# Decoder trunk: operand sums, negated copies, one softmax scaling and one rotation table put in other places

## The chip, the cores and the metric

The kernel runs on one core of a Trainium2 chip. The metric is the device time of one execution in microseconds (us); the median of several runs counts. The engines are PE (TensorE: matmuls and transposes), DVE (VectorE), ACT (ScalarE), POOL (GpSimd) and SP (SyncE, here only a DMA queue). Each engine works through its own instruction queue in order; ACT, POOL and SP also issue DMAs from theirs.

## The reference, cut to what matters

One layer with two groups of eight heads on a sequence of 1024 tokens, model width 2048, all in float32:

```python
hn = rmsnorm(h, norm_mix_g)
sb_q, sb_k, sb_v, sb_g, df_q, df_k, df_v, df_g = split(hn @ w_in)
sb_out = stick_breaking_attention(sb_q, sb_k, sb_v)               # 8 heads of 128
dq, dk = partial_rope(df_q, pos), partial_rope(df_k, pos)
df_out = softmax1(dq, dk) @ df_v - lam * softmax2(dq, dk) @ df_v  # 8 heads, 2 x 64
df_out = rmsnorm(df_out, subln_g) * (1 - lambda_init)
mixed = concat([sb_out * silu(sb_g), df_out * silu(df_g)])
h = h + mixed @ w_out
gate = sigmoid(rmsnorm(h, norm_ple_g) @ w_ple_gate)
out = rmsnorm(h + gate * (p @ w_ple_proj), norm_final_g)
```

## The kernel before

Activations are kept transposed: features on partitions, tokens along the free axis, in two halves of 512 tokens (half 1 first, since attention is causal and the tokens stand in reverse order). Each float32 operand of a big product is split into a high part that TensorE can use exactly and a low rest. ACT makes the high part (a cast or a scaled copy), DVE the low part (source minus high part), and a product is three matmuls: high by high, high by low, low by high. So nearly every matmul needs one ACT step and then one DVE step to have been done.

The time falls into these parts:

- **The ramp, 0 to about 100 us.** The value and gate columns of `w_in` (16 units) are multiplied by a seven-product scheme on 2 x 2 blocks: A11, A12, S1 to S4 and A22 name the activation operands, of which S1 to S4 are sums and differences of blocks. The ramp does A11 and A12 for all units, two units at a time: A11 of both, then A12 of both. For each unit `load` fetches the weights and `cast` makes `wfh` (ACT, L714) and `wfl` (DVE, L715); the casts for the next two units stand behind the two A12 products. The other operands are formed in between: `todo` is a queue of 40 small steps (`combine`, `divide`, `split1`) that work on tiles `x`, and `some(n)` writes the next n of them into the queues of ACT and DVE at that place of the program.
- **The other products of this scheme**, to about 615 us.
- **Head units, about 615 to 1600 us.** For each half (1, then 0) and each of the 16 heads, in the order of `ORDER`: differential head 8, stick-breaking head 0, 9, 1, and so on to 15, 7. A unit makes q and k of one head with 96 matmuls (L295 to L297), in 32 groups of three. In between, the attention of the head before is run.
- **Output projection, gate, final norm**, from about 1600 us, again by seven products.

The order of the work in a unit is a table, `TICK`. After each group of three matmuls `side.tick()` counts on by one and writes out the steps whose time has come; `side.later(dt, fn)` puts a step dt ticks on. So a table entry moves a step along the queues of ACT and DVE, relative to the matmuls and to the other steps. PE, DVE and ACT keep exactly this order; the queues of POOL and SP are set by a scheduler.

At the **seam** between the halves, three things meet. The last units of half 1 end their attention. `mixed` stores each head's gated output `sg` and, for half 1, a negated copy `neg` (ACT, L327), which goes by DMA into the block sums for the output projection. And the activations of half 0 take the place of those of half 1: `swap(pc)`, at ticks 7, 15, 23 and 31 of the last unit, loads four tiles each, and `split` in `load_x0` makes `xh` (ACT, L1245) and `xl` (DVE, L1246) as many ticks later as `TICK["x0"]` says. In the same place the rotation table `cs` of half 0 (cosine and sine, 128 x 1024) is loaded by POOL and multiplied by the row norms on DVE (L1227). The table of half 1 is scaled in the same way near 642 us.

In the attention of a differential head, `weights` runs per block of 128 rows and per softmax c: `top` (DVE, L426) finds the row maximum of the scores `z`, `one` (ACT, L434) takes the exponential into `et`, and for c = 1 `two` scales `et` by lam over the row sum (DVE L439 and L440, then ACT L441), and `three` (DVE, L446) forms the difference, which PE then turns (L481, tile `tp`). ACT and DVE split the turned blocks into `awh` and `awl` (L500, L505; `lead` for the first block, L499, L504) for the product with the values (`av`, L523 to L528). A score tile `z` is free for the next scores when L434 has read it. The ticks of `top`, `one`, `two` and `three` are `TICK["df_soft"]`.

Of the kernel before, what the change touches and what calls it, by code (L numbers as in the profile page):

```python
# [17 lines left out]
ALU = mybir.AluOpType  # L18
AX = mybir.AxisListType

P = 128
D = 2048
S = 1024
HALF = 512
# [15 lines left out]
TICK = {  # L40
    "sumlag": 2, "gvx": ((22, 27), (80, 85)), "chore": (36, 78, 87), "opx": (8, 12), "turn": 76, "lag": 15, "gap": (4, 6),
    "parts": (1, 2), "vparts": (3, 4), "sums": (0, 2), "squared": (3, 4.5), "norm": (1, 4),
    "df_scores": (-20, -16, -13, -8, -4, 0, 4, 8), "df_turn": (19, 19), "df_v": -1, "df_norm": 44.5,
    "sb_scores": (-2, 5.5, 13.5, 22), "sb_turn": (32, 36), "sb_v": 23, "df_soft": (1, 1.5, 4, 5.5),
    "sb_stick": (1, 1, 3, 5.5), "taken": (28, 31), "sb_split": (1, 2), "kv": 9, "df_vg": (25, 37, 42, 58, 59.5),
    "sb_vg": (4, 15, 16, 24, 25.5), "q_turn": (-1.0, 5.5, 5, 6.5, 10, 12, 13.5),
# [5 lines left out]
    "begun": (86.5, 91.5, 93.5, 94.5, 93.5), "mid_turn": 76, "mid_lag": 17, "mid_gap": (4, 6),  # L52
    "mid_df_scores": (-20, -16, -9, -8.5, -1, -0.5, 4, 8), "mid_df_turn": (19, 17), "mid_df_v": -1, "mid_df_norm": 44.5,
    "mid_sb_scores": (-3, 5, 12.5, 21), "mid_sb_turn": (32, 36), "mid_sb_v": 22, "mid_taken": (28, 31),
    "mid_q_turn": (-1.5, 4.5, 4.5, 5.5, 9.5, 11.5, 12.5), "mid_k_turn": (-1.5, 8, 8.5, 9, 13.5, 15, 16, 17.5), "end_turn": 76,
    "end_lag": 15, "end_gap": (4, 6), "end_df_scores": (-23, -16, -15, -8, -4, 0, 4, 8), "end_df_turn": (18.5, 19),
    "end_df_v": -1, "end_df_norm": 44.5, "end_sb_scores": (-2, 6, 13.5, 22), "end_sb_turn": (32, 36), "end_sb_v": 23,
    "end_taken": (28, 31), "end_q_turn": (-1.0, 5, 5, 6.5, 10, 12, 13.5),
    "end_k_turn": (-4.5, 8, 8.5, 10, 13.5, 15, 16, 17.5),
}  # L60
# [9 lines left out]
def _body(ctx, nc, tc, ap):  # L70
# [247 lines left out]
    def mixed(half, hd, t):  # L318


        ph, second, i = hd % H // 4, hd < H, hd % 4
        S1, S2, S3, S4 = [comb_d[ph, j, i] for j in range(4)]
        if half == 1 or second:
            nc.sync.dma_start(mixed_d[half, hd], t)
        if half == 1:
            n = ev.tile([P, HALF], F32, name="neg", tag="xt", bufs=4)
            A.activation(n, t, AF.Copy, scale=-1.0)  # L327
# [12 lines left out]
        G.dma_start(S4, t, accum_op=ALU.add)  # L340


    def attention(at, pz, half, hd, q, qz, K, KL, VV, sg, vg, rcol):

        sb = hd < H
        nkey = HALF * len(K)
        nb = nkey // P
# [12 lines left out]
        def scores(c, rb):  # L360
# [29 lines left out]

            side.later(TICK["sb_stick"][0], masked)
            return z

        def weights(rb, c):
# [3 lines left out]
            if sb:  # L398
                def one():
                    pt = at.tile([P, S], F32, name="pt", tag="pt")  # L400
                    bt = row_block("bt", rb)
                    A.activation(pt[:, off + 1:nkey], z[:, off:nkey - 1], AF.Sigmoid, scale=rcol[:, 0, rb:rb + 1])  # L402
                    A.activation(bt[:, vw], z[:, vw], AF.Sigmoid, scale=rcol[:, 1, rb:rb + 1])
                    ws[rb] = pt, bt

                def two():
                    pt, bt = ws[rb]
                    w = slice(off + 1, nkey)
                    V.tensor_tensor_scan(pt[:, w], pt[:, w], pt[:, w], initial=1.0, op0=ALU.mult, op1=ALU.bypass)  # L409
# [6 lines left out]
                for dt, fn in zip(TICK["sb_stick"][1:], (one, two, three)):  # L416
                    side.later(dt, fn)
                return

            def top():  # L420
# [5 lines left out]
                V.tensor_tensor_reduce(z[:, vw], z[:, vw], add, -DF_SCALE, 3.0e38, ALU.add, ALU.min, mx)  # L426
                side.later(TICK["df_soft"][1], partial(one, mx))

# [58 lines left out]
        def parts(pr, g, tp, wh, wl):  # L487
# [18 lines left out]

            side.later(TICK["parts"][0], high)
            side.later(TICK["parts"][1], low)

        def mix(pr, g):  # L510
# [27 lines left out]
            av = sm.rearrange("p a b -> p (a b)")  # L538
            side.later(TICK["sums"][0], lambda: A.copy(sm[:, 1, :], av4[:, 3, :]))

# [6 lines left out]

            side.later(TICK["sums"][1], summed)
            if sb or pr == 0:
# [16 lines left out]

            side.later(TICK["squared"][0], squared)
            side.later(TICK["squared"][1], low)

# [51 lines left out]
    with tc.tile_pool(name="at", bufs=2) as at, tc.tile_pool(name="pz", bufs=2, space=PSUM) as pz:  # L621
# [313 lines left out]
        def some(n):  # L935
            for _ in range(n):
                if todo:
                    todo.popleft()()

        for u in range(0, NVG, 2):  # L940
            aa = [pp.tile([P, HALF], F32, name="pa", tag="acc", bufs=2) for _ in range(2)]
            for i in range(2):
# [20 lines left out]
                if u:  # L963
                    some(4)
            for i in range(2):
# [260 lines left out]
        def scale_rope(hf, cs):  # L1226
            V.tensor_tensor(cs, cs, rstds[hf].unsqueeze(1).to_broadcast([P, 2, HALF]), op=ALU.mult)  # L1227

# [178 lines left out]
        for half in (1, 0):  # L1407
            X = X0 if half == 0 else X1

            for hd in ORDER:  # L1410
# [15 lines left out]
                if half == 1 and hd == ORDER[-1]:  # L1426
# [3 lines left out]

                    side.add([(8 * pc + 7, partial(swap, pc)) for pc in range(4)])

# [107 lines left out]
                if half == 1 and hd == ORDER[-2]:  # L1540
                    cs = rope_of(0)
                    side.add([(27, partial(scale_rope, 0, cs))])
                if hd >= H:
# [860 lines left out]
```

## Time and profile before

| | us |
|---|---|
| median of 3 runs | 2325.04 (2324.98 to 2326.09) |
| the profiled execution, its own time | 2326.05 |
| its span from the first to the last instruction | 2324.3 |
| PE busy | 2306.5 |
| DVE busy | 1796.6 |
| ACT busy | 1269.1 |
| POOL busy | 326.1 |

The granted clock of TensorE was 0.999 in this execution. In rows of the timeline the columns are: start, duration, engine, line, operation, output <- inputs, shape, count; in brackets stands the time that the engine was idle just before, and what ended it. "PEld" is the loading of weights into the array, which runs beside the matmuls. "SPq" marks DMA issues.

### The profile page before, as it was taken

To read this page: it belongs to the slowest core of one execution; us is meant where nothing else is said; L and a number is where in the kernel's file an instruction comes from. 1 tells how busy PE (TensorE), PEld (TensorE's weight loads), DVE (VectorE), ACT (ScalarE), POOL (GpSimd) and SP (SyncE) were. 2 spreads that over 40 slices of the span, in tenths; PEclk is the share of its full clock that TensorE was granted. 3 is DMA by queue.
4 is the path that set the end of the run, shared out by engine and by line. 5 is a ranking of instruction groups with operands and counts; after the bars stand their busy time and mean duration, and the time that the engine had idled before them with its cause. 6 is when DMAs were issued, how large, how long until landed. Compare 5 with 4: busy or idle time off the path is not lost. (4 is left out here: it accounts for less than half of the span.)

```text
span 2324.3 us, 32653 instructions
## 1 busy us (share of the span) xinstructions
PE 2306.5 (99%) x11089; PEld 1928.1 (83%) x11089; DVE 1796.6 (77%) x3119; ACT 1269.1 (55%) x2303; POOL 326.1 (14%) x497
## 2 busy tenths in 40 slices
PE   9999999999999999999999999999999999999998
PEld 7888888888888888887888888888888888888887
DVE  7487776766578888877778878788787988687787
ACT  6323243333356677777776776667733435542555
POOL 2121111111211111100011001110121121111000
PEclk9999999999999999999999999999999999999999
DMA  7586788876888787888676667777899789998975
GB/s 265 201 303 227 253 280 220 222 160 129 208 265 259 242 255 246 253 287 284 203 214 186 182 207 207 205 200 243 259 216 242 248 248 282 309 358 267 299 255 187
DMA packets 258455, 556.66 MB, mean 239 GB/s; under 512 B 28896, under 2 KB 39392, under 8 KB 258288
## 3 DMA queue, kind: packets, MB, share of 16 engines
q1 hardware_dynamic: 180816, 366.55, 49.9%
q0 software_dynamic: 60912, 158.10, 25.7%
q10 hardware_dynamic: 16560, 29.92, 3.6%
q8 instruction: 87, 1.43, 0.2%
q14 instruction: 80, 0.66, 0.1%
HBM read 359.16 MB, written 203.69 MB: 242 GB/s over the span
## 5 line engine op out<-in xcount | busy, mean ns | idle before, releaser
L788 ACT CAST wpr<-T 128x512 fp32r<-128x512 f32 x208 | 127.1, 620 | 470.7 <-DVE T L747 393.7
L295 PE MATMUL acc<-xh,whi 128*128 128x512 f32 x768 | 312.9, 407 | 0.0
L297 PE MATMUL acc<-xh,wlo 128*128 128x512 f32 x768 | 301.1, 392 | 0.1
L296 PE MATMUL acc<-xl,whi 128*128 128x512 f32 x768 | 300.7, 392 | 0.0
L297 PEld LDWEIGHTS acc<-xh,wlo 128*128 128x128 f32 x768 | 144.2, 188 | 32.5 <-DVE wlo L196 0.5
L295 PEld LDWEIGHTS acc<-xh,whi 128*128 128x128 f32 x768 | 144.7, 188 | 24.5 <-issue 0.2
L296 PEld LDWEIGHTS acc<-xl,whi 128*128 128x128 f32 x768 | 144.9, 189 | 23.8 <-issue 0.2
L901 POOL DMA_DIRECT2D vg_d<-hc x128 | 89.1, 696 | 447.0 <-DVE hc L1119 263.4
L802 DVE TENSOR_TENSOR wpr<-T,wpr 128x512 fp32r<-128x512 f32 x208 | 142.6, 685 | 6.9 <-ACT wpr L788 3.8
L200 ACT CAST whi<-wraw 128x1024 fp32r<-128x1024 f32 x128 | 134.1, 1048 | 18.2 <-DMA wraw<-w_in 8.4
L788 ACT CAST wpr<-wraw 128x512 fp32r<-128x512 f32 x128 | 78.8, 617 | 105.1 <-DMA wraw<-tw_d 31.8
L434 ACT ACTIVATE et<-z,mx 128x512 f32<-128x512 f32 (+7 forms) x128 | 95.2, 744 | 60.3 <-DVE mx L426 60.2
L426 DVE CUSTOM_DVE_ANT_0 z<-z,wide 128x512 f32<-128x512 f32 (+7 forms) x128 | 97.6, 764 | 29.9 <-PE z L379 27.1
L505 DVE TENSOR_TENSOR awl<-tp,awh 128x256 fp32r<-128x256 f32 (+1 forms) x160 | 92.5, 578 | 33.9 <-ACT awh L500 33.0
L500 ACT CAST awh<-tp 128x256 fp32r<-128x256 f32 (+1 forms) x160 | 80.6, 504 | 43.7 <-PE tp L481 42.7
L802 DVE TENSOR_TENSOR wpr<-wraw,wpr 128x512 fp32r<-128x512 f32 x128 | 86.7, 685 | 16.4 <-ACT wpr L788 16.3
L409 DVE TENSOR_TENSOR_SCAN pt<-pt 128x511 f32<-128x511 f32 (+3 forms) x64 | 86.7, 1355 | 14.4 <-ACT pt L402 13.9
L196 DVE TENSOR_TENSOR wlo<-wraw,whi 128x1024 fp32r<-128x1024 f32 x56 | 68.5, 1224 | 14.2 <-ACT whi L200 13.7
L528 PE MATMUL av<-awl,v 128*128 128x256 f32 x256 | 72.6, 284 | 0.4 <-DVE awl L505 0.4
L526 PE MATMUL av<-awh,v 128*128 128x256 f32 x256 | 72.2, 282 | 0.5 <-ACT awh L500 0.4
L527 PE MATMUL av<-awh,v 128*128 128x256 f32 x256 | 72.2, 282 | 0.0
L441 ACT ACTIVATE et<-et,l 128x512 f32<-128x512 f32 (+3 forms) x64 | 49.4, 772 | 40.9 <-DVE l L440 40.8
(581 smaller groups left out, 6937.8 us busy)
## 6 DMA issues: line engine op xcount, KB each, us to landing
wraw<-w_in SPq DMA_DIRECT2D x128, 512.0 KB, 4.7
wraw<-w_vg SPq DMA_DIRECT2D x143, 256.0 KB, 3.8
vg_d<-hc POOLq DMA_DIRECT2D x128, 256.0 KB, 5.0
wlo_d<-wlo POOLq DMA_DIRECT2D x56, 512.0 KB, 6.4
wlo<-wlo_d SPq DMA_DIRECT2D x48, 512.0 KB, 3.8
wraw<-w_gate SPq DMA_DIRECT2D x92, 256.0 KB, 5.6
h_d<-hc POOLq DMA_DIRECT2D x56, 256.0 KB, 5.4
wraw<-w_out SPq DMA_DIRECT2D x56, 256.0 KB, 4.7
```

Of the source, the lines that this page charges most:

```text
L200: side.later(1, lambda: A.copy(hi[:, o], raw[:, o]))
L295: T.matmul(acc[c], hi[:, k2, kh, c, :], xh, start=first, stop=False)
L296: T.matmul(acc[c], hi[:, k2, kh, c, :], xl, start=False, stop=False)
L297: T.matmul(acc[c], lo[k2][:, kh, c, :], xh, start=False, stop=last)
L409: V.tensor_tensor_scan(pt[:, w], pt[:, w], pt[:, w], initial=1.0, op0=ALU.mult, op1=ALU.bypass)
L426: V.tensor_tensor_reduce(z[:, vw], z[:, vw], add, -DF_SCALE, 3.0e38, ALU.add, ALU.min, mx)
L434: A.activation(et[:, vw], z[:, vw], AF.Exp, bias=mx[:, 0:1], scale=-1.0, accum_out=l[:, c:c + 1])
L500: A.copy(wh[:, o, :], tp[:, o, :])
L505: V.tensor_tensor(wl[:, o, :], tp[:, o, :], wh[:, o, :].bitcast(F32), op=ALU.subtract)
L788: A.copy(t[:, 0], src)
L802: V.tensor_tensor(t[:, 1], src, t[:, 0].bitcast(F32), op=ALU.subtract)
L901: G.dma_start(vg_d[hf, blk, u], o, **(dict(accum_op=ALU.add) if ph else {}))
```

## The change

Five edits, in four groups:

1. In the ramp, from the second pair of units on, `some(4)` behind an A11 product becomes `some(3)`, and `some(2)` behind an A12 product becomes `some(1)` (`some(3)` becomes `some(2)` in the last pair). The 40 steps and their order among each other stay.
2. The negated copy of half 1 is put two ticks on (`side.later(TICK["neg"], negated)`), together with its DMAs.
3. The steps of `weights` take their ticks from the table of the seam, where it has an entry (`tk`). One entry is added, `end_df_soft`: in the last differential head of half 0 the scaling `two` comes at 4.5 ticks instead of 4.
4. The rotation table of half 0 is scaled by POOL instead of DVE. And the third and fourth operand of the third group of `load_x0` are split at 15 and 16 ticks instead of 13 and 14.

```diff
 TICK = {
+    "neg": 2, "cs": 27, "x0_at": (7, 7, 7, 7), "end_df_soft": (1, 1.5, 4.5, 5.5),
...
-    "x0": ((5, 5, 13, 12), (5, 6, 13, 14), (5, 6, 13, 14), (5, 5, 13, 11)),
+    "x0": ((5, 5, 13, 12), (5, 6, 13, 14), (5, 6, 15, 16), (5, 5, 13, 11)),
...
-        if half == 1:
+        def negated():
             n = ev.tile([P, HALF], F32, name="neg", tag="xt", bufs=4)
             A.activation(n, t, AF.Copy, scale=-1.0)
             if second:
...
             else:
                 for d in (S2, S3, S4):
                     nc.sync.dma_start(d, n)
+
+        if half == 1:
+            side.later(TICK["neg"], negated)
             return
...
+        seam = ("mid_" if half else "end_") if hd in ORDER[-2:] else ""
+
+        def tk(nm):
+            return TICK.get(seam + nm, TICK[nm])
+
...
-            side.later(TICK["df_soft"][0], top)
+            side.later(tk("df_soft")[0], top)
             if c:
-                side.later(TICK["df_soft"][2], two)
-                side.later(TICK["df_soft"][3], three)
+                side.later(tk("df_soft")[2], two)
+                side.later(tk("df_soft")[3], three)
...
                 if u:
-                    some(4)
+                    some(3)
...
-                some(2 if u < NVG - 2 else 3)
+                some(1 if u < NVG - 2 else 2)
...
-            V.tensor_tensor(cs, cs, rstds[hf].unsqueeze(1).to_broadcast([P, 2, HALF]), op=ALU.mult)
+            (V if hf else G).tensor_tensor(cs, cs, rstds[hf].unsqueeze(1).to_broadcast([P, 2, HALF]), op=ALU.mult)
```

What this does to the queues is shown at three places. The matmuls keep their order throughout. Lines of the changed kernel are numbered up to 8 differently, since the table and `mixed` have other lengths: L715 becomes L722, L1245 becomes L1252, L327 becomes L326, L441 becomes L448.

The ramp, DVE, before: the steps around the casts of the third pair's weights (`wfl`); the other rows are operand steps, where `x` and `cS` with their numbers are tiles of the second pair of blocks.

```order
L678 SCALAR_TENSOR_TENSOR cA_346<-x_115,gvec,cA_346 128x512
L890 SCALAR_TENSOR_TENSOR x_115<-x_115,gvec 128x512
L892 TENSOR_TENSOR x_115<-x_115,x_111 128x512
L893 SCALAR_TENSOR_TENSOR x_111<-x_111,gneg,x_115 128x512
L715 TENSOR_TENSOR wfl<-wraw,wfh 128x512 x2
L894 SCALAR_TENSOR_TENSOR x_111<-x_111,gneg 128x512
L676 TENSOR_TENSOR cS2l<-x_111,cS2h 128x512
L715 TENSOR_TENSOR wfl<-wraw,wfh 128x512 x2
```

The same steps on DVE in the changed kernel:

```order
L722 TENSOR_TENSOR wfl<-wraw,wfh 128x512 x2
L685 SCALAR_TENSOR_TENSOR cA_365<-x_115,gvec,cA_365 128x512
L722 TENSOR_TENSOR wfl<-wraw,wfh 128x512 x2
L897 SCALAR_TENSOR_TENSOR x_115<-x_115,gvec 128x512
L899 TENSOR_TENSOR x_115<-x_115,x_111 128x512
L900 SCALAR_TENSOR_TENSOR x_111<-x_111,gneg,x_115 128x512
L901 SCALAR_TENSOR_TENSOR x_111<-x_111,gneg 128x512
L683 TENSOR_TENSOR cS2l<-x_111,cS2h 128x512
```

Four operand steps stood ahead of the first two low parts, and two more ahead of the next two; now none and one.

The seam, ACT, before: from the end of the last differential head's norm (`avb`, half 1) on; `xh` with numbers are operands of half 0, `neg` the first of two negated copies, `et` the exponential that frees a score tile.

```order
L578 ACTIVATE avb<-avb 128x512
L434 ACTIVATE et,l<-z,mx 128x512
L1456 COPY qk<-acc_9638 128x512
L327 ACTIVATE neg<-sg 128x512
L1245 ACTIVATE xh_9793<-xl_9794,gvec 128x512
L1245 ACTIVATE xh_9880<-xl_9881,gvec 128x512
L1472 CAST q<-qk 128x512
L1245 ACTIVATE xh_9796<-xl_9797,gvec 128x512
L1245 ACTIVATE xh_9883<-xl_9884,gvec 128x512
L434 ACTIVATE et,l<-z,mx 128x512
```

And in the changed kernel:

```order
L585 ACTIVATE avb<-avb 128x512
L441 ACTIVATE et,l<-z,mx 128x512
L1463 COPY qk<-acc_9638 128x512
L1252 ACTIVATE xh_9793<-xl_9794,gvec 128x512
L1252 ACTIVATE xh_9880<-xl_9881,gvec 128x512
L1479 CAST q<-qk 128x512
L1252 ACTIVATE xh_9796<-xl_9797,gvec 128x512
L1252 ACTIVATE xh_9883<-xl_9884,gvec 128x512
L326 ACTIVATE neg<-sg 128x512
L441 ACTIVATE et,l<-z,mx 128x512
```

The copy moved behind four operand casts and the cast of q. A little further on, the second copy moved behind a weight cast (`whi`), and the casts of the third group's last two operands moved behind two exponentials and behind the scaling L441. On POOL the multiply of `cs` stands right behind the load of `cs`, with an instruction that names no operands between them (shown as ISA), and ahead of the stores of k.

The start of the output projection, ACT, before: the attention of the last differential head (half 0) among the first casts of the projection (`cA12h`).

```order
L434 ACTIVATE et,l<-z,mx 128x896
L441 ACTIVATE et<-et,l 128x1024
L500 CAST awh<-tp 128x512
L1472 CAST k<-qk 128x512
L670 CAST cA12h<-cA12l 128x512
L1560 COPY hc<-pa 128x512
```

And in the changed kernel:

```order
L441 ACTIVATE et,l<-z,mx 128x896
L507 CAST awh<-tp 128x512
L1479 CAST k<-qk 128x512
L448 ACTIVATE et<-et,l 128x1024
L677 CAST cA12h<-cA12l 128x512
L1567 COPY hc<-pa 128x512
```

The scaling of `et` (L441, now L448) moved behind the cast of the turned weights and that of k. It is the only ACT step that this entry moves.

More of the change, by code (lines that the diff above doesn't have):

```diff
@@ L40 @@
 TICK = {
[L41 to L45, printed above, removed]
@@ L56 @@
[L56 to L59, printed above, removed]
+    "neg": 2, "cs": 27, "x0_at": (7, 7, 7, 7), "end_df_soft": (1, 1.5, 4.5, 5.5), "sumlag": 2, "gvx": ((22, 27), (80, 85)),
+    "chore": (36, 78, 87), "opx": (8, 12), "turn": 76, "lag": 15, "gap": (4, 6), "parts": (1, 2), "vparts": (3, 4), "sums":
@@ new lines @@
+    (0, 2), "squared": (3, 4.5), "norm": (1, 4), "df_scores": (-20, -16, -13, -8, -4, 0, 4, 8), "df_turn": (19, 19), "df_v":
+    -1, "df_norm": 44.5, "sb_scores": (-2, 5.5, 13.5, 22), "sb_turn": (32, 36), "sb_v": 23, "df_soft": (1, 1.5, 4, 5.5),
+    "sb_stick": (1, 1, 3, 5.5), "taken": (28, 31), "sb_split": (1, 2), "kv": 9, "df_vg": (25, 37, 42, 58, 59.5), "sb_vg":
+    (4, 15, 16, 24, 25.5), "q_turn": (-1.0, 5.5, 5, 6.5, 10, 12, 13.5), "k_turn": (-4.5, 8, 8.5, 10, 13.5, 15, 16, 17.5),
[4 rows of a table added]
+    (18, 21.5, 22, 25, 25.5, 33, 33.5, 38, 42, 46, 50, 54, 58, 62, 66, 70), "begun": (86.5, 91.5, 93.5, 94.5, 93.5),
@@ L389, in masked @@
                 V.tensor_tensor(z[:, rs], z[:, rs], mask, op=ALU.add)
-            side.later(TICK["sb_stick"][0], masked)
+            side.later(tk("sb_stick")[0], masked)
             return z
@@ L414, in three @@
                     ws[rb] = bt
-                for dt, fn in zip(TICK["sb_stick"][1:], (one, two, three)):
+                for dt, fn in zip(tk("sb_stick")[1:], (one, two, three)):
                     side.later(dt, fn)
@@ L426, in top @@
                 V.tensor_tensor_reduce(z[:, vw], z[:, vw], add, -DF_SCALE, 3.0e38, ALU.add, ALU.min, mx)
-                side.later(TICK["df_soft"][1], partial(one, mx))
+                side.later(tk("df_soft")[1], partial(one, mx))
             def one(mx):
@@ L505, in low @@
                 V.tensor_tensor(wl[:, o, :], tp[:, o, :], wh[:, o, :].bitcast(F32), op=ALU.subtract)
-            side.later(TICK["parts"][0], high)
-            side.later(TICK["parts"][1], low)
+            side.later(tk("parts")[0], high)
+            side.later(tk("parts")[1], low)
         def mix(pr, g):
@@ L538, in mix @@
             av = sm.rearrange("p a b -> p (a b)")
-            side.later(TICK["sums"][0], lambda: A.copy(sm[:, 1, :], av4[:, 3, :]))
+            side.later(tk("sums")[0], lambda: A.copy(sm[:, 1, :], av4[:, 3, :]))
             def summed():
@@ L546, in summed @@
                         mixed(half, hd, sg)
-            side.later(TICK["sums"][1], summed)
+            side.later(tk("sums")[1], summed)
             if sb or pr == 0:
@@ L565, in low @@
                 sqs[0] = both, sq, sqh, sql
-            side.later(TICK["squared"][0], squared)
-            side.later(TICK["squared"][1], low)
+            side.later(tk("squared")[0], squared)
+            side.later(tk("squared")[1], low)
         def norm():
@@ L1429, in swap @@
                             side.add([(TICK["x0"][pc][i], load_x0(kt))])
-                    side.add([(8 * pc + 7, partial(swap, pc)) for pc in range(4)])
+                    side.add([(8 * pc + TICK["x0_at"][pc], partial(swap, pc)) for pc in range(4)])
                 def store_k(hd=hd, qk=qk, half=half):
```

14 lines of the change are left out of this document (8 added, 6 removed), and 9 rows, old and new, of the table TICK.

## The prediction

> **What bounds the kernel now.** I read the page's busy times first, then the stages, then PE's waits in the stages where it is not full, then each such place in the timeline.
>
> ```profile
> PE 2306.5 (99%) x11089; PEld 1928.1 (83%) x11089; DVE 1796.6 (77%) x3119; ACT 1269.1 (55%) x2303; POOL 326.1 (14%) x497
> 19.02:64.78 45.76, 44.96 (x194) 35.66 (x192) 33.38 (x51) 29.66 (x54) 10.77 (x20) 1.00 0.76 256
> 1060.70:1083.00 22.30, 18.34 (x89) 13.94 (x88) 18.62 (x47) 16.51 (x37) 2.68 (x4) 1.00 0.91 299
> 1618.60:1640.00 21.40, 20.82 (x112) 17.36 (x111) 18.86 (x40) 16.06 (x32) 4.83 (x6) 1.00 1.08 311
> ```
>
> The first row gives each engine's busy time; the others have the stretch, its length, busy time of PE, PEld, DVE, ACT and POOL, the clock, the DMA share and GB/s. PE is the bound: 2306.5 of 2324.3 us. The change removes no matmul, so it can give back only waits of PE. Three stretches hold waits that its edits touch: the ramp (19 to 65 us), the seam between the halves (1060.7 to 1083: 3.96 idle) and the start of the output projection (0.58 idle). Everywhere else I expect PE to keep its pace.
>
> Idle time understates a wait. A 512-column matmul lasts 0.39 us, but one starts every 0.227, so I count by starts:
>
> ```profile
> 19.02 0.39 PE L691 MATMUL pa<-cA11h,wfh 128*128 128x512 f32 x1
> 64.78 0.39 PE L691 MATMUL pa<-cA11h,wfh 128*128 128x512 f32 x1
> 75.66 0.39 PE L691 MATMUL pa<-cA11h,wfh 128*128 128x512 f32 x1
> 20.09 0.73 ACT L889 ACTIVATE x<-x,gvec 128x512 f32<-128x512 f32 x1 [0.88 <-DVE cA L678]
> 21.18 1.14 ACT L714 CAST wfh<-wraw 128x512 fp32r<-128x512 f32 x2
> 29.24 1.14 ACT L714 CAST wfh<-wraw 128x512 fp32r<-128x512 f32 x2
> 30.42 0.75 DVE L893 SCALAR_TENSOR_TENSOR x<-x,gneg,x 128x512 f32<-128x512 f32 x1
> 31.09 1.29 DVE L715 TENSOR_TENSOR wfl<-wraw,wfh 128x512 fp32r<-128x512 f32 x2
> 31.82 0.50 PE L693 MATMUL pa<-cA11h,wfl 128*128 128x512 f32 x1 [0.78 <-DVE wfl L715]
> ```
>
> **Fewer operand-sum steps in the ramp.** These rows are starts of pairs of units. Undisturbed, a pair takes 75.66 - 64.78 = 10.88 us. The four pairs from 19.02 to 64.78 took 45.76 against 43.52: 2.24 lost. The causes stand in the other rows. At 20.09 an operand step holds ACT for DVE, and the weight casts come only at 21.18. At 29.24 the casts are made, but DVE works on operand sums until 31.09 before it takes the weights' low parts, and PE waits to 31.82. With 3 + 1 steps where 4 + 2 stood, the casts and low parts stand ahead of those steps: the low part due at 31.09 can start when the first cast ends, 29.24 + 0.57 = 29.8, and end about 30.5, ahead of PE. I take the whole **2.2**, with 1.0 as the lower end (the largest wait alone). The steps themselves are not fewer: 40 in all, done 8 a pair instead of 12, so they end in the pair that starts near 54 instead of the one near 43. DVE is busy 33.38 of 45.76 there, so it has room. The four loads that reuse their buffers move along SP:
>
> ```profile
> 49.16 3.30 SPq L994 DMA_DIRECT2D xv<-xT  x3
> 53.88 25.29 SPq L706 DMA_DIRECT2D wraw<-w_vg  x12
> ```
>
> SP is in order, and weights stand behind them. The second such load now waits for a step of about 59 us; the weights behind it wait for a cast of about 62 anyway (estimates from the pair length of 10.88), so it costs nothing while that 3 us of cover lasts.
>
> **The seam: negated copy, rotation table, two late operands.**
>
> ```profile
> 1054.58 0.64 ACT L578 ACTIVATE avb<-avb 128x512 f32<-128x512 f32 x1
> 1055.78 0.58 ACT L1456 COPY qk<-acc 128x512 f32<-128x512 f32 x1
> 1058.39 0.63 ACT L327 ACTIVATE neg<-sg 128x512 f32<-128x512 f32 x1 [2.03 <-DVE sg L584]
> 1058.93 1.32 ACT L1245 ACTIVATE xh<-xl,gvec 128x512 fp32r<-128x512 f32 x2
> 1054.36 1.22 DVE L1227 TENSOR_TENSOR cs<-cs,ssa 128x1024 f32<-128x1024 f32 x1
> 1055.50 0.68 DVE L581 SCALAR_TENSOR_TENSOR sqv<-msq,avb 128x512 f32<-128x512 f32 x1
> 1057.66 0.69 DVE L584 TENSOR_TENSOR sg<-sg,avb 128x512 f32<-128x512 f32 x1
> 1059.67 1.42 DVE L1246 SCALAR_TENSOR_TENSOR xl<-xl,gvec,xh 128x512 fp32r<-128x512 f32 x2 [1.31 <-ACT xh L1245]
> 1060.89 0.34 PE L379 MATMUL z<-kl,qz 128*128 128x384 f32 x1
> 1062.71 0.45 PE L378 MATMUL z<-k,q 128*128 128x384 f32 x1 [1.48 <-ACT et L434]
> 1065.77 0.29 DVE L504 TENSOR_TENSOR lead<-tp,lead 128x128 fp32r<-128x128 f32 x1 [1.27 <-ACT awh L500]
> 1066.11 0.50 PE L523 MATMUL av<-lead,v 128*128 128x256 f32 x2 [1.28 <-DVE lead L504]
> 1073.01 0.61 DVE L446 SCALAR_TENSOR_TENSOR et<-et,l 128x384 f32<-128x384 f32 x1
> 1073.68 0.33 PE L481 MATMUL tp<-ident,et 128*128 128x128 f32 x1 [0.55 <-DVE et L446]
> 1077.16 0.38 PE L372 MATMUL z<-k,q 128*128 128x256 f32 x1 [0.38 <-ACT et L434]
> 1079.29 0.39 PE L523 MATMUL av<-lead,v 128*128 128x256 f32 x1 [0.23 <-DVE v L466]
> ```
>
> The table's multiply leaves DVE (1.22), but L581 also needs ACT's L578, which ends at 1055.22: it can move only from 1055.50 to 1055.25, so this edit is worth 0.25 and L584 ends at 1058.10. The copy is worth more. At 1058.39 ACT had stood 2.03 us for it, with the operand casts queued behind, and DVE stood 1.31 for those. Behind the casts, ACT can take them from 1056.4, and DVE's low parts start when L584 ends: 1058.10 for 1059.67, so 1.57 earlier. From there to the lead at 1065.77 DVE waits only once, for a chain that starts from its own result, so everything shifts together: the et that PE's z waits for, that z from 1062.71 to its due time of 1061.06 (0.17 after 1060.89), the lead to 1064.2, PE's L523 to **1064.55**. The first wait goes (1.65), but the second stays at 1.5, since PE now arrives earlier too. Next late is L446. The third and fourth operands of the third group move two ticks later, and one of their DVE steps now stands ahead of L446, its cast behind ACT's scaling: 0.68 + 0.4, less the 0.68 taken away earlier. I put L446's successor at 1072.6 for 1073.68, 1.1 earlier. The second copy now stands behind a weight cast and the et at L434 comes 2 us earlier, so the wait at 1077.16 goes; the one at 1079.29 shrinks to 0.1. The seam ends **1.8** earlier: 0.3 if the operand casts find their data late, 5.0 if every wait goes (3.96 idle, plus about 0.2 of overlap for each of five).
>
> The multiply now runs on GpSimd, of which this trace shows no arithmetic:
>
> ```profile
> L1405 POOL MEMSET qz<- x1: 964/964/964, 605.5 to 605.5; 128x1024 f32 x1
> 1039.77 0.72 POOL L1223 DMA_DIRECT2D cs<-rope  x1 [11.69 <-DVE qk L1514]
> DMA to landing us min/median/max: 5.0/5.7/6.4
> 1049.65 0.75 DVE L1246 SCALAR_TENSOR_TENSOR xl<-xl,gvec,xh 128x512 fp32r<-128x512 f32 x1 [1.36 <-DMA wlo<-wlo_d]
> 1094.64 0.71 DVE L1514 TENSOR_TENSOR qk<-qk,cs 128x512 f32<-128x512 f32 x1
> ```
>
> One pass over 1024 columns is 0.96; with two reads and a write I bound it by 0.96 and 2.9 and take 2.3, near the upper end. The table lands at about 1045.5, the multiply ends near 1048, and its first reader is at 1094.64: 46 us of cover. Queued behind it on POOL is the store of keys, which nobody needs in this half. In the 1.36 us before 1049.65 DVE stands for a DMA, so even a blocked step has room there. The Trainium skill ("SBUF — State Buffer", "Who interferes with whom") says that a DVE instruction with two SBUF inputs and a GpSimd instruction that reads SBUF exclude each other for a whole instruction. No run here shows it yet; by that rule this edit could cost DVE the multiply's length where the two meet, the third rival.
>
> **Last pair's scaling.**
>
> ```profile
> 1620.65 1.15 ACT L441 ACTIVATE et<-et,l 128x1024 f32<-128x1024 f32 x1 [0.37 <-DVE l L440]
> 1621.71 0.56 ACT L500 CAST awh<-tp 128x512 fp32r<-128x512 f32 x1
> 1622.32 0.39 PE L526 MATMUL av<-awh,v 128*128 128x256 f32 x1 [0.36 <-ACT awh L500]
> 1623.05 0.39 PE L528 MATMUL av<-awl,v 128*128 128x256 f32 x1 [0.22 <-DVE awl L505]
> ```
>
> With the awh cast ahead of the 1.15 us scaling, it starts at about 1620.3 (0.37 before the scaling does now), and its low part is done at 1621.5, before PE comes at 1621.8. By starts the two waits are 0.5 and 0.4, with two slow restarts of 0.1: **1.1**. The scaling ends 0.6 later, but its reader on DVE stands behind another cast that ends earlier, so nothing is late.
>
> **Sum.** 2.2 + 1.8 + 1.1 = 5.1. The profiled execution took 2326.05, 1.75 outside its span; less 5.1 it is 2320.95. That execution is 1.0 above the median of 2325.04, so against the median: **2319.9**. Something like 0.2% (4.65 us) is what a measurement of this kernel can tell from no change.
>
> **The rivals.**
> 1. *All waits of the seam go* (5.0): 8.3 in all, 2316.7. For it: one late chain causes the first. Against it: DVE's queue has no gap from 1058 to 1065. Chance 0.13.
> 2. *The operand casts find no data.* The seam's DMA engines are full (0.91 of the stretch); if loads hold ACT as the copy did, the seam gives 0.3: 3.6 in all, 2321.4. Against it: ACT had them ready at 1058.93 without a wait for DMA. Chance 0.13.
> 3. *GpSimd's multiply holds DVE.* If it starts not at 1046 but between 1050 and 1055, where DVE works without a gap, DVE loses up to 2.9 before L581, which had 0.7 to spare: the seam gives 1.8 - 2.2, in all 2.9, 2322.1. Chance 0.12.
> 4. *Slower: the multiply comes late.* A bare instruction without operands precedes it on POOL, and no row prices it. Should it hold POOL past 1096.6 (first reader plus some 2 us of slack), DVE and then PE stand for every further us; past 1106 the kernel is slower by over 0.2%. A hold of 70 us from 1040 ends at 1110 and gives 13.4 - 5.1: 2333.3. Against it: the cover of 46 us, of which the multiply takes at most 2.9. Chance 0.07.
>
> **How the numbers follow.** The forecast has 0.55. Its terms range over 1.0 to 2.4, 1.0 to 3.0 and 0.8 to 1.1: over 4.65 in three cases of four (0.42), else within 0.2% (0.13). With rival 1, faster has 0.55; with rivals 2 and 3, the same has 0.38; rival 4 is slower, 0.07. The range from 2317.5 to 2322.2 takes in the forecast, rivals 2 and 3 and half of rival 1.
>
> **What would show it.** Right: pairs of 10.88 from 19 us on; no wait at z L378, the wait at lead L504 still 1.2 or more; awh ahead of the scaling and no wait after it; a GpSimd multiply ending before 1050. Wrong: PE waits in the ramp, a seam whose idle time is above 3.5 or below 1, or DVE gaps released by POOL.

## The result, and the profile after

The changed kernel takes 2321.03 us (median of 22 runs, 2320.35 to 2322.64), the kernel before 2325.30 us (22 runs, 2323.93 to 2327.81). The ratio is 0.9982, with a 95% interval of 0.9976 to 0.9987: 4.3 us less by the medians, 3.0 to 5.6 by the interval. The forecast was 2319.9 (2317.5 to 2322.2) and 5.1 us. The profiled execution took 2320.39, with a span of 2318.3, beside 2326.05 and 2324.3.

The page's busy times, then three stretches of the changed kernel (stretch, length, busy time of PE, PEld, DVE, ACT, POOL, clock, DMA share, GB/s): the four pairs of the ramp, the seam from its score products on, and 4 us inside it.

```profile
PE 2303.3 (99%) x11089; PEld 1928.5 (83%) x11089; DVE 1795.6 (77%) x3118; ACT 1269.6 (55%) x2303; POOL 329.8 (14%) x498
18.55:62.07 43.52, 43.52 (x194) 36.05 (x193) 32.60 (x50) 29.35 (x53) 10.77 (x20) 1.00 0.74 257
1057.86:1079.00 21.14, 18.48 (x95) 14.90 (x94) 17.68 (x46) 14.90 (x35) 2.65 (x4) 1.00 1.04 333
1069.70:1073.70 4.00, 3.90 (x18) 3.27 (x19) 3.80 (x11) 3.34 (x10) 0.88 (x1) 1.00 1.07 279
```

PE has no idle time left in the ramp; in the seam 21.14 - 18.48 = 2.66 are left of 3.96 (in a stretch of 22.30 there). The rows of the timeline that answer to those of the prediction, first the ramp:

```profile
18.49 0.39 PE L698 MATMUL pa<-cA11h,wfh 128*128 128x512 f32 x1
62.01 0.39 PE L698 MATMUL pa<-cA11h,wfh 128*128 128x512 f32 x1
27.34 1.14 ACT L721 CAST wfh<-wraw 128x512 fp32r<-128x512 f32 x2
27.99 1.29 DVE L722 TENSOR_TENSOR wfl<-wraw,wfh 128x512 fp32r<-128x512 f32 x2 [0.82 <-ACT wfh L721]
160.33 0.50 PE L698 MATMUL pbc<-cA,wpr 128*128 128x512 f32 x1 [0.24 <-DVE u L1164]
```

The first two rows are starts of pairs, four pairs apart: 43.52, or 10.88 a pair (the stretch above is as long, and PE is busy in all of it). DVE takes the low parts as soon as the first cast is made (27.34 + 0.57, 27.99). The last row is new: at 160 us PE now waits for DVE. Then the seam:

```profile
1053.50 1.34 ACT L1252 ACTIVATE xh<-xl,gvec 128x512 fp32r<-128x512 f32 x2
1056.48 0.63 ACT L326 ACTIVATE neg<-sg 128x512 f32<-128x512 f32 x1
1052.50 0.69 DVE L588 SCALAR_TENSOR_TENSOR sqv<-msq,avb 128x512 f32<-128x512 f32 x1 [0.75 <-ACT avb L585]
1054.67 0.69 DVE L591 TENSOR_TENSOR sg<-sg,avb 128x512 f32<-128x512 f32 x1
1055.29 1.41 DVE L1253 SCALAR_TENSOR_TENSOR xl<-xl,gvec,xh 128x512 fp32r<-128x512 f32 x2
1058.15 0.34 PE L386 MATMUL z<-kl,qz 128*128 128x384 f32 x1
1058.33 0.34 PE L385 MATMUL z<-k,q 128*128 128x384 f32 x1
1061.72 0.51 PE L530 MATMUL av<-lead,v 128*128 128x256 f32 x2 [1.37 <-DVE lead L511]
1068.47 0.75 DVE L1253 SCALAR_TENSOR_TENSOR xl<-xl,gvec,xh 128x512 fp32r<-128x512 f32 x1 [0.43 <-ACT xh L1252]
1069.14 0.61 DVE L453 SCALAR_TENSOR_TENSOR et<-et,l 128x384 f32<-128x384 f32 x1
1069.80 0.33 PE L488 MATMUL tp<-ident,et 128*128 128x128 f32 x1 [1.29 <-DVE et L453]
1044.22 2.40 POOL L1234 TENSOR_TENSOR cs<-cs,ssa 128x1024 f32<-128x1024 f32 x1 [6.47 <-DMA cs<-rope]
1044.32 0.69 DVE L512 TENSOR_TENSOR awl<-tp,awh 128x512 fp32r<-128x512 f32 x1 [1.12 <-ACT awh L507]
1114.95 0.34 PE L386 MATMUL z<-kl,qz 128*128 128x384 f32 x1
```

ACT casts before it copies, DVE goes from L591 to the operands without a gap, and the two score products follow each other (1058.15, 1058.33) where the second had come 1.82 later (1060.89, 1062.71). The wait for the lead part stays (1.37), the one before the transposes has grown (1.29 for 0.55). The last row is the same score product in the next differential head. In the kernel before it is this one:

```profile
1119.74 0.34 PE L379 MATMUL z<-kl,qz 128*128 128x384 f32 x1
```

So from score product to score product it was 1119.74 - 1060.89 = 58.85 and is now 1114.95 - 1058.15 = 56.80: 2.05 us gained. I use this distance as the measure of the seam below. At the start of the projection the scaling L448 now stands behind the cast of awh, and the product with it comes without a wait:

```profile
1615.38 0.58 ACT L507 CAST awh<-tp 128x512 fp32r<-128x512 f32 x1
1616.36 1.16 ACT L448 ACTIVATE et<-et,l 128x1024 f32<-128x1024 f32 x1
1617.00 0.28 PE L533 MATMUL av<-awh,v 128*128 128x256 f32 x1
1631.41 0.66 PE L530 MATMUL av<-lead,v 128*128 128x256 f32 x2
```

In the last row two matmuls take 0.66 together where they took 0.39 before: a small wait, 0.25 by starts. The second of them needs `v`, whose low part DVE ends at 1631.63.

### The profile page after: what moved, and what is told of

Same layout as the page of the kernel before. It is cut to its first block, busy times and chain, and to the rows that moved or that the text cites. A ratio compares the mean times of both kernels' runs of the same rounds, so it can differ in the third digit from the quotient of the medians.

```text
span 2318.3 us, 32647 instructions
## 1 busy us (share of the span) xinstructions
PE 2303.3 (99%) x11089; PEld 1928.5 (83%) x11089; DVE 1795.6 (77%) x3118; ACT 1269.6 (55%) x2303; POOL 329.8 (14%) x498
## 4 chain that ended last, share of the span: by engine, by line
PE 96%; DVE 1%; DMA 1%; ACT 1%; issue 0%; SPq 0%; DVEq 0%; ACTq 0%
PE acc L294 10%; PE acc L296 10%; PE acc L295 10%; PE pbc L698 5%; PE pbc L700 5%; PE pbc L699 4%; PE pa L699 4%; PE pa L700 4%; PE pa L698 4%; PE pc L698 3%; PE pc L700 3%; PE pc L699 3%; PE tp L488 3%; PE pb L1839 2%; PE pb L1840 2%; PE pb L1841 2%
## 5 line engine op out<-in xcount | busy, mean ns | idle before, releaser
L795 ACT CAST wpr<-T 128x512 fp32r<-128x512 f32 x208 | 127.1, 621 | 475.7 <-DVE T L754 394.1
L795 ACT CAST wpr<-wraw 128x512 fp32r<-128x512 f32 x128 | 78.9, 618 | 107.3 <-DMA wraw<-tw_d 36.7
L441 ACT ACTIVATE et<-z,mx 128x512 f32<-128x512 f32 (+7 forms) x128 | 95.1, 743 | 57.9 <-DVE mx L433 57.7
L512 DVE TENSOR_TENSOR awl<-tp,awh 128x256 fp32r<-128x256 f32 (+1 forms) x160 | 92.5, 578 | 32.4 <-ACT awh L507 31.4
L416 DVE TENSOR_TENSOR_SCAN pt<-pt 128x511 f32<-128x511 f32 (+3 forms) x64 | 86.7, 1354 | 14.4 <-ACT pt L409 13.9
L448 ACT ACTIVATE et<-et,l 128x512 f32<-128x512 f32 (+3 forms) x64 | 49.5, 774 | 42.4 <-DVE l L447 42.4
```

What stands on the lines that cost most here:

```text
L441: A.activation(et[:, vw], z[:, vw], AF.Exp, bias=mx[:, 0:1], scale=-1.0, accum_out=l[:, c:c + 1])
L512: V.tensor_tensor(wl[:, o, :], tp[:, o, :], wh[:, o, :].bitcast(F32), op=ALU.subtract)
L795: A.copy(t[:, 0], src)
```

## The experiments

Times are medians, each beside the kernel before in the same runs (2325.27 to 2325.45); the changed kernel is 2321.03. An interval of a single comparison is about 2 us to either side, so the places are read from the traces.

**The edits alone.** The ramp, on the kernel before:

```diff
-                    some(4)
+                    some(3)
...
-                some(2 if u < NVG - 2 else 3)
+                some(1 if u < NVG - 2 else 2)
```

> The kernel before, with edit 1 alone (3 and 1 operand steps where 4 and 2 stood). My theory: the waits between 19 and 65 us go, four pairs of units take 43.5 us instead of 45.8, and the time falls by 2.2 us (1.0 to 2.4), to about 2323.1 beside 2325.3. Rival: the gain of the profiled pair of runs at the start was partly the start itself (the first 19 us differed by 0.5 us between the two traces), and the operand steps or the loads that move later are paid for between 65 and 100 us: less than 1.0 us.

2323.44 beside 2325.27 (ratio 0.9990, 0.9982 to 0.9999). The start of the four pairs and that of the pair behind them, and a wait of PE:

```profile
18.75 0.39 PE L691 MATMUL pa<-cA11h,wfh 128*128 128x512 f32 x1
62.27 0.39 PE L691 MATMUL pa<-cA11h,wfh 128*128 128x512 f32 x1
160.60 0.50 PE L691 MATMUL pbc<-cA,wpr 128*128 128x512 f32 x1 [0.25 <-DVE u L1157]
```

From 18.75 to 62.27 are 43.52 us: all 2.24 us came, as my theory said. Nothing was paid back between 65 and 100 us, but the wait at 160 us is there with this edit alone: the matmul starts 0.41 late by starts, where it had been 0.13 late, so 0.3 is lost there.

The negated copy, on the kernel before, for all units of half 1:

```diff
-        if half == 1:
+        def negated():
...
+        if half == 1:
+            side.later(2, negated)
```

> The kernel before, with edit 2 alone (negated copy two ticks later). My theory: the copy was what held ACT, so this edit alone takes away the wait of the scores z at 1062.7 (1.65 us by starts), leaves the one for the lead part at 1.4 to 1.5, and gives 1.3 to 1.6 of the seam's 2.05 us: about 2323.8 beside 2325.3. Rival: the rotation table's multiply, still on DVE here, is what holds the chain; then the z wait stays above 1 us and the gain is at most 0.3 us.

2324.46 beside 2325.27 (0.9995, 0.9986 to 1.0004). The distance is 57.13: 1.72 gained. PE's waits between 1050 and 1100 us (waiting and awaited step, us, times, longest; line numbers are 3 higher than in the kernel before):

```profile
PE av L526 <- DVE lead L507: 1.4, 1, 1.4
PE tp L484 <- DVE et L449: 0.6, 1, 0.6
PE av L526 <- DVE v L469: 0.2, 1, 0.2
```

Both waits for scores are gone, the 1.48 and the later 0.38 (at 1077.16 in the kernel before); the one for the lead part is 1.37 for 1.28, the other two are as they were. The copy was the cause, not the table.

The scaling in the last differential head, on the kernel before:

```diff
-                side.later(TICK["df_soft"][2], two)
+                side.later(4.5 if half == 0 and hd == ORDER[-2] else TICK["df_soft"][2], two)
```

> The kernel before, with the table entry for the last differential head alone (scaling at 4.5 ticks). My theory: the two waits at 1622.3 and 1623.1 go, PE gains 1.1 us there and nothing else moves: about 2324.2 beside 2325.3. Rival: the scaling, now behind a cast, makes a later step late, and half or more of the 1.1 us comes back as a wait between 1625 and 1650: a gain under 0.6 us.

2324.52 beside 2325.27 (0.9997, 0.9989 to 1.0006): too small for the times. In the trace the two waits are gone; the first product with awh, the one that had waited at 1622.32:

```profile
1620.30 0.28 PE L526 MATMUL av<-awh,v 128*128 128x256 f32 x1
```

By starts 1.1 goes there, and 0.25 comes back at the next block's lead product, as in the changed kernel. Between theory and rival: most of the gain stays.

**The two small edits, undone in the changed kernel.** First the late operands:

```diff
-    "x0": ((5, 5, 13, 12), (5, 6, 13, 14), (5, 6, 15, 16), (5, 5, 13, 11)),
+    "x0": ((5, 5, 13, 12), (5, 6, 13, 14), (5, 6, 13, 14), (5, 5, 13, 11)),
```

> The changed kernel, with the two late operand splits of the third group back at 13 and 14 ticks. My theory: at 15 and 16 one DVE step stands between the sums and the softmax difference at 1069.1 and waits 0.43 us for a cast that stands behind the scaling on ACT; put back, that difference ends about 0.7 us earlier, the wait for it before the transposes at 1070.1 falls from 1.46 to about 0.75, and the time is 0.5 to 0.8 us lower than the changed kernel's: about 2320.4. Rival: at 13 and 14 the two casts wait for their data or delay the chain to the lead part, the wait at 1062.1 grows above 1.53, and the time is 0.3 us or more above the changed kernel's.

2320.48 (ratio to before 0.9980, 0.9971 to 0.9989, which takes in the changed kernel's). The distance is 56.83, as with the edit (56.80).

```profile
PE av L530 <- DVE lead L511: 1.3, 1, 1.3
PE tp L488 <- DVE et L453: 0.6, 1, 0.6
PE av L530 <- DVE v L473: 0.2, 1, 0.2
```

Half of my theory held: the wait before the transposes fell from 1.3 to 0.6. But the one for the values, which the changed kernel lost, came back, and smaller ones with it. The median lies where my theory put it, but 0.55 below the changed kernel's is within the interval, and the distance doesn't show it. The edit only exchanges waits; it neither gives nor costs anything that these traces show.

The rotation table back on DVE:

```diff
-            (V if hf else G).tensor_tensor(cs, cs, rstds[hf].unsqueeze(1).to_broadcast([P, 2, HALF]), op=ALU.mult)
+            V.tensor_tensor(cs, cs, rstds[hf].unsqueeze(1).to_broadcast([P, 2, HALF]), op=ALU.mult)
```

> The changed kernel, with the rotation table of half 0 multiplied on DVE again. My theory: DVE waits for ACT's avb (the second step of the norm) anyway, so the multiply on DVE costs only what sticks out behind that, 0.25 to 0.3 us of the seam: about 2321.3 beside the changed kernel's 2321.0. Rival: its 1.2 us stand in full on the chain to the lead part; then the wait at 1062.1 grows from 1.5 to above 2.3 and the time is 0.8 us or more above the changed kernel's.

2320.69 (0.9981, 0.9972 to 0.9990): no difference in the times. The distance is 57.10, so the edit is worth 0.30 in the seam.

```profile
1050.87 1.22 DVE L1234 TENSOR_TENSOR cs<-cs,ssa 128x1024 f32<-128x1024 f32 x1
1052.01 0.68 DVE L588 SCALAR_TENSOR_TENSOR sqv<-msq,avb 128x512 f32<-128x512 f32 x1
```

The multiply fills the time in which DVE waits for ACT (0.75 at 1052.50 in the changed kernel), so only what sticks out counts, as the prediction had it.

**Does GpSimd's arithmetic hold DVE?** Rival 3 did not show in the changed kernel, so I made the two meet. The six passes add and subtract the same row, so the table keeps its values but for rounding:

```diff
+            if hf == 0:
+                for o in 3 * (ALU.add, ALU.subtract):
+                    G.tensor_tensor(cs, cs, rstds[hf].unsqueeze(1).to_broadcast([P, 2, HALF]), op=o)
```

> The changed kernel, with six more passes of the same form (add and subtract of the row norms, by turns) on GpSimd behind the table's multiply, so that GpSimd works from about 1044 to 1061, beside the dense stretch of DVE from 1052.5 to 1060 (most of its steps there have two inputs in SBUF). If the two exclude each other for a whole instruction (rival 3 of the prediction), DVE's steps there get longer or wait up to 2.4 us each time, or GpSimd's passes get longer than 2.40; the chain to the lead part is delayed, and the wait at 1062.1 grows from 1.5 by 2 to 7 us. If not, DVE's steps keep 0.69 and 0.75 us, GpSimd's passes 2.40, and the time stays within 0.5 us of the changed kernel's 2321.0.

2332.78 beside 2325.45 (1.0031, 1.0019 to 1.0044): 11.8 us above the changed kernel. The timeline, and one stretch (the passes are L1237; L1256 is L1253 of the changed kernel):

```profile
1044.59 2.40 POOL L1234 TENSOR_TENSOR cs<-cs,ssa 128x1024 f32<-128x1024 f32 x1 [5.76 <-DMA cs<-rope]
1047.60 2.48 POOL L1237 TENSOR_TENSOR cs<-cs,ssa 128x1024 f32<-128x1024 f32 x1
1050.58 13.14 POOL L1237 TENSOR_TENSOR cs<-cs,ssa 128x1024 f32<-128x1024 f32 x5
1045.40 0.69 DVE L512 TENSOR_TENSOR awl<-tp,awh 128x512 fp32r<-128x512 f32 x1 [1.13 <-ACT awh L507]
1047.98 2.65 DVE L1256 SCALAR_TENSOR_TENSOR xl<-xl,gvec,xh 128x512 fp32r<-128x512 f32 x1 [1.36 <-DMA wlo<-wlo_d]
1053.21 8.31 DVE L1256 SCALAR_TENSOR_TENSOR xl<-xl,gvec,xh 128x512 fp32r<-128x512 f32 x3
1061.45 2.42 DVE L420 TENSOR_TENSOR bt<-pt,bt 128x127 f32<-128x127 f32 x1
1059.90:1070.14 10.24, 4.24 (x11) 3.17 (x12) 10.10 (x15) 4.64 (x9) 3.74 (x2) 0.50 0.14 52
1064.39 0.90 PE L488 MATMUL tp<-ident,bt 128*128 128x128 f32 x3 [8.26 <-DVE sm L549]
```

An operand step takes 2.65 to 2.8 us where it takes 0.75, a 127-column product 2.42 where it takes 0.3, and the running product between them (L416, which reads one SBUF tile as both inputs) 2.73 where it takes 0.41. Each ends 0.15 to 0.55 us after a pass has ended. GpSimd is held much less: its passes took 2.40 to 2.67. The step L512, one of whose inputs (tp) lies in PSUM, keeps its 0.69 beside the first multiply. The six DVE steps took 16.3 us for 3.7, 2.1 of delay each. DVE fell over 12 us behind, and PE stood 8.26.

So rival 3's mechanism is real. Its price of 2.2 was another sum, though (a multiply of at most 2.9 less 0.7 to spare), so that 11.8 us for six passes, 2.0 each, comes close to it is chance. And not all of the 11.8 is the hold itself: while PE stood, its clock fell to 0.50 (last but one row), and eight matmuls from 1066.80 on took 3.5 us for 1.8. The changed kernel escapes the hold by its place: from 1044.2 to 1046.6 DVE has only steps that read a PSUM tile (L512 at 1044.32, then two on a score tile z), and idle time.

**What the seam's remaining waits are worth.** Two waits of 1.3 to 1.4 are left. First the lead part's, whose cast stands on ACT behind a scaling that waits for DVE:

```diff
+    "mid_df_soft": (1, 1.5, 4.5, 5.5),
```

> The changed kernel, with the scaling at 4.5 ticks in the last differential head of half 1 too (an entry mid_df_soft like end_df_soft), so that the casts of the turned block for the lead part stand ahead of the scaling on ACT. My theory: the lead cast stands on ACT behind a scaling that waits 1.55 us for DVE; ahead of it, the lead part is done at about 1060.5 and its wait of 1.53 us goes. The scaling then comes behind a weight cast, so the softmax difference is ready only some 0.5 us earlier, and the wait before the transposes at 1070.1 grows from 1.46 to 2 to 2.5. Net gain 0.4 to 1.0 us: about 2320.3. Rival: the whole gain comes back at the transposes, since the chain through the difference is what PE follows; then the time stays at 2321.0 within 0.2.

2322.66 (0.9989, 0.9980 to 0.9998), above the changed kernel; the distance is 58.72, 1.9 more. The wait for the lead is gone, and there is one of 2.93 before the transposes. The PE rows around its end, and a stretch:

```profile
1072.29 0.33 PE L488 MATMUL tp<-ident,et 128*128 128x128 f32 x1 [2.93 <-DVE et L453]
1073.29 0.63 PE L294 MATMUL acc<-xh,whi 128*128 128x512 f32 x1
1072.98:1076.39 3.41, 3.41 (x10) 2.63 (x9) 3.36 (x10) 2.54 (x9) 0.59 (x1) 0.50 1.03 252
```

My theory fell, and the rival had only half of it. The whole wait came back at the transposes, as the rival said, and then the clock fell: 0.50 for 3.41 us from 1072.98 on, when PE was at work again. There a matmul lasts 0.63 for 0.39, and eight of them start 0.43 apart instead of 0.227, so some 1.6 us are lost. In the changed kernel, with two waits of 1.37 and 1.29 some 7 us apart, the clock stays at 1.00. Here one long wait was dearer than two short ones of about the same sum.

The profiled execution took 2324.77, 2.1 above the median of its kernel. It also has a wait of 1.14 at 614 us, far from this edit, that the changed kernel's trace doesn't have. The distance leaves that out: its 1.9 is close to the 1.6 between the medians. Whether the clock fell in the other ten executions isn't shown.

With the late operands back at 13 and 14 ticks as well:

> As the run before, and the two late operand splits of the third group back at 13 and 14 ticks. My theory: with the lead wait gone, the difference for the transposes is next late, and without the operand step ahead of it it ends 0.7 us earlier: 0.5 us or more below the run before, about 2319.7. Rival: the two exchange waits as they did without the scaling's move (the wait that goes at the transposes comes back at the scores and the values behind them), and the time is the same as the run before within 0.2.

2321.69 (0.9983, 0.9974 to 0.9992), distance 58.12. Two waits stand close together, and the clock falls too:

```profile
1067.77 0.44 PE L488 MATMUL tp<-ident,et 128*128 128x128 f32 x2 [0.69 <-DVE sm L549]
1069.86 0.36 PE L488 MATMUL tp<-ident,et 128*128 128x128 f32 x1 [1.65 <-DVE et L453]
1070.02:1073.44 3.42, 3.42 (x10) 2.65 (x10) 2.56 (x8) 3.23 (x11) 0.88 (x1) 0.50 0.85 240
```

The 0.6 us below the run before (by the distance; 1.0 by the medians) is as expected in sign and size; the level is not.

Next the second block's chain was brought forward as well:

```diff
-    "x0": ((5, 5, 13, 12), (5, 6, 13, 14), (5, 6, 15, 16), (5, 5, 13, 11)),
+    "x0": ((5, 5, 13, 12), (5, 6, 13, 14), (5, 6, 17, 18), (5, 5, 13, 11)),
...
-                side.later(tk("df_soft")[2], two)
-                side.later(tk("df_soft")[3], three)
+                side.later({0: 4.5, 1: 3}.get(rb if half == 1 and hd == ORDER[-2] else None, tk("df_soft")[2]), two)
+                side.later({1: 5}.get(rb if half == 1 and hd == ORDER[-2] else None, tk("df_soft")[3]), three)
```

> The changed kernel, in the last differential head of half 1 with the scaling of the first block at 4.5 ticks (behind the lead cast), that of the second block at 3 ticks and its softmax difference at 5, and the two late operand splits of the third group at 17 and 18 ticks, so that on DVE they stand behind that difference. My theory: a wait of PE in the seam is worth what its whole chain gives; with the lead cast ahead of the scaling (as in the two runs before) and the next late chain (row sums, scaling, difference of the second block) freed of the operand steps, the difference ends at about 1067.5 instead of 1069.8, the waits of 1.53 and 1.46 us both go but for about 0.5, PE is never idle long enough to lose its clock, and the seam's 3.8 us fall to 1.5 to 2.5: about 2319.4. Rival: the operand steps that are put behind the difference, or the steps behind them, are then late for the scores and values of the third block, PE waits there as long as before, and the time is 2321 or above.

2321.02 (0.9980, 0.9971 to 0.9989), the changed kernel's time; distance 56.58. PE's two longest waits in the seam:

```profile
PE z L379 <- ACT et L441: 1.4, 1, 1.4
PE tp L488 <- DVE et L453: 0.4, 1, 0.4
```

Both waits are gone or small, and a new one of 1.4 stands at the third block's scores (and 0.25 at its values): the rival. Its variant with the splits at 16.5 and 17 ticks (and the difference at 4.5):

> As the run before, but with the two operand splits at 16.5 and 17 ticks: one DVE order in which both stand directly behind the difference, and the second negated copy behind both of their casts on ACT. My theory: within 0.4 us of the run before, since only steps without a near reader change places: about 2319.4. Rival: the order of the steps behind the difference decides when the third block's scores are free, and the two differ by more than 0.5 us.

2320.77 (0.9980, 0.9971 to 0.9989), distance 56.53: the same as the run before, as expected of the two beside each other, but not at the level expected.

Last, the operands of the fourth group were moved out of this stretch, with the second block early (first; shown against that kernel) and, second, with its steps and the third group's operands at the ticks of the kernel before (13 and 14):

```diff
-    "x0": ((5, 5, 13, 12), (5, 6, 13, 14), (5, 6, 17, 18), (5, 5, 13, 11)),
+    "x0": ((5, 5, 13, 12), (5, 6, 13, 14), (5, 6, 17, 18), (16, 17, 20, 19)),
```

> As the kernel with the second block early (third group's late operands at 17 and 18 ticks), and the operand splits of the fourth group at 16, 17, 20 and 19 ticks instead of 5, 5, 13 and 11: PE reads them only from about 1079 on, after the third block of the attention. My theory: in the seam DVE's queue is full from 1055 to 1076, so every wait taken away came back behind it; only steps taken out of that stretch count. Four steps (2.8 us of DVE) leave the time ahead of the third block's scores; the wait of 1.61 us for these at 1072.3 and the 0.56 before the transposes go, the one for the values (0.4) stays, the seam's 3.5 to 3.8 us fall to 0.8 to 1.5, and the time is about 2318.4. Rival: the four operands are now late for PE, which waits for their low parts between 1078 and 1085 by 1.5 us or more, and the time stays at 2320.5 or above.

> As the run before, but the third group's late operands at 13 and 14 ticks and the second block's scaling and difference at their old 4 and 5.5 ticks (only the first block's scaling is moved to 4.5). My theory: the operand steps fill the time in which DVE waits for the row sums, the difference ends at about 1067.5 as in the kernel with the second block early, the wait before the transposes is about 0.6, the one for the third block's scores is gone: 0.3 to 0.5 us above the run before, about 2318.8. Rival as there: PE waits between 1078 and 1085, 2320.5 or above.

2322.39 (0.9988, 0.9979 to 0.9997) and 2321.77 (0.9984, 0.9976 to 0.9993), distances 58.60 and 57.59. PE's three longest waits from 1050 to 1100 us in the first:

```profile
PE acc L294 <- ACT qk L1493: 1.6, 1, 1.6
PE vps L468 <- ACT et L441: 1.0, 1, 1.0
PE av L535 <- DVE awl L512: 0.8, 1, 0.8
```

In both, the waits moved again, now behind the third block: to the low part awl, behind the moved operands on DVE, and to the copy that frees an accumulator. My theory that steps taken out of the stretch must count was half right: up to 1075 only a wait of 0.40 is left (0.55 in the second), and they cost more after it. The rival had the level right (2320.5 or above), but PE waits at awl and at the accumulator, not for the moved operands themselves. None of these variants is measurably faster than the changed kernel.

## Why the prediction was right, and where it was not

**The sum.** Forecast 5.1. By starts in the traces: ramp 2.24, seam 2.05, projection 1.1, less 0.3 at 160 us and 0.25 at the next lead product: 4.8. The median says 4.3, its interval 3.0 to 5.6. The profiled pair differs by 5.66; of that 0.53 is the start (the first of the four pairs begins at 18.49 for 19.02). The first edit takes a few steps out there too, behind the A12 products of the pair before, but this start lies between 18.0 and 19.0 us in the three traces without the edit and between 17.9 and 19.8 in the eleven with it, so the 0.53 can't be put down to it. That the sum comes out so close is in part luck: what the seam gave beyond its forecast is set off against two small waits that weren't foreseen. The size was right to within what the runs tell, and the difference lies just inside the 0.2% (4.65) that I had set as the bound, not beyond it as the forecast had it.

**The ramp.** Right, 2.24 for 2.2, by the cause named: alone it gives the same 43.52. The loads that move along SP cost PE nothing in the ramp. Missed: the wait at 160 us. Why DVE is late there by some 0.3 us wasn't settled: the changed kernel's trace leads back to an ACT cast (L795) at 150.91, which starts 0.37 us after DVE has made its input, for 0.09 in the kernel before; what it waits for is open.

**The seam.** 2.05 for 1.8, and by the steps named. Measured from the score product ahead of the first wait, the score product behind that wait comes 1.64 earlier (forecast 1.65), the lead's product 1.65 (1.56) and the transposes 1.14 (1.1). Alone, the copy gives 1.72 and the table 0.30 (forecast 0.25); the late operands give 0, where the forecast had them delay L446 by 0.4. That the wait for the lead part stays, since PE comes earlier too, is what the trace shows (1.37), and that the difference L446, now L453, becomes the late one also (1.29; the forecast's own times give 1.0).

**The projection.** 1.1 went, but 0.85 stayed: the step "nothing is late" failed. PE comes 1.12 earlier, but DVE only 0.65, since it waits 0.79 for a cast (cA12h, L677) that now stands behind the scaling on ACT. The values of the next block had been done 0.38 ahead of their product; now PE meets them before DVE has them.

**The rivals.** The waits of the seam did not all go. (One argument against that rival was misread: DVE's queue does have a gap after 1058, the 1.31 us before 1059.67 that the prediction's own row shows; from there to 1064.5 it is full.) The last six runs show why: each wait is the end of a chain through ACT's and DVE's queues (DVE is busy 17.68 of 21.14 there), and a wait that is taken away comes back at the next step of that chain. The operand casts found their data (1053.50, no wait). The multiply ended at 1046.62, before 1050; the instruction ahead of it held nothing. That GpSimd can hold DVE was right; that the price per pass came out near the forecast's 2.2 was chance. It didn't happen in the changed kernel because the multiply met steps that read PSUM. The prediction had asked only whether DVE would be busy, not what its steps read.

## What to carry to other kernels

Price a wait by the whole in-order chain that ends it, and ask at once which wait is next: of the seam's five, only the one whose cause stood idle on its engine (a copy that waited while four casts were ready) was worth its full length, and taking it away took a second, shorter one with it. Taking away the lead's or the transposes' wait gave nothing that could be measured. Before a step goes to GpSimd, look at what DVE does in those microseconds, not at how free GpSimd is. And don't join small waits of TensorE into a long one: in the two traces where that happened, the clock fell.

## What the runs showed of the hardware

- **DVE steps with two inputs in SBUF wait for a whole GpSimd instruction that reads SBUF.** They took 2.4 to 2.8 us beside passes of 2.4 to 2.7 us, for 0.3 to 0.75 alone; a step with a PSUM input kept its 0.69. GpSimd lost at most 0.3 us a pass. The Trainium skill ("SBUF — State Buffer", "Who interferes with whom") states that the two exclude each other for a whole instruction; on DVE's side the trace agrees.
- **Waits of TensorE well under 4 us can halve its clock.** A wait of 2.93, and waits of 0.69 and 1.65 with two transposes between, were each followed by 3.4 us at 0.50; in and after the wait of 8.26 it was 0.50 for 10.24 us. Two waits of 1.3 to 1.4, 7 us apart, and single ones of up to 1.56 were not. Where between these the limit lies isn't shown. The Trainium skill ("TensorE: Matmul & The Clock Gate", Part 1) gives an idle window of about 3.4 us on a free-running count; 2.93, and 2.34 in two parts, were enough here.
- **A GpSimd multiply of 128x1024 with two inputs** took 2.40 us, for 1.22 on DVE.
